# Attention logits as three rounded products, and the key weights' staging moved in the queue

## The chip, the cores and the metric

The kernel runs on one core of a Trainium2 chip. The metric is the device time of one execution in microseconds (us). Before the change three runs gave 1312.15, 1314.40 and 1316.61 us, a median of 1314.4 us. The profile is that of one further execution.

The engines are TensorE (PE; PEld is its weight loading), VectorE (DVE), ScalarE (ACT), GpSimd (POOL) and SyncE (SP), which here only issues DMAs. Each works through a queue of its own in order.

## The reference, cut to what matters

A decoder trunk of two layers on 512 tokens of width 1024, in float32. Layer 0 is a Mamba-2 mixer and a ConvFFN. Then keys and values are projected once. Layer 1 is differential attention (8 heads, two maps of 64 dimensions each, causal) and a second ConvFFN:

```
k_sh, v_sh = rms_norm(kv[..., :1024] per 64, k_norm_g), kv[..., 1024:]
q = rms_norm((rms_norm(x, ln_g) @ q_w) per 64, q_norm_g)
logits = einsum('bqhcd,bkhcd->bhcqk', q, k) / 8 + bias        # c: the two maps
p = softmax(where(causal, logits, -inf))
o = einsum('bhqk,bkhd->bqhd', p[:, :, 0] - lam * p[:, :, 1], v)
```

## The kernel before, in words

Most products are made in a rounded form of float32 (type F32R): an operand is split into a high half, rounded by an ACT copy, and a low half, the rest, made on DVE, and a product of two operands is three matmuls (high by high, high by low, low by high) that add up in one PSUM bank. Weights come as pieces of 1024 columns by 128 partitions: a load on SP, the split, three buffers ahead of PE (`Weights`, `chunk`). Logits, attention values and transposes are plain float32 matmuls.

The order of PE's instructions is written out by hand. The instructions of ACT, DVE, POOL and the DMA queues are put in order by a planner, which issues each once its inputs are expected to be ready. It may place an instruction much earlier than the program has it. `tc.issue_after(i)` keeps what is inside it behind instruction i in the planned order.

**Layer 0's ConvFFN** (`ffn`) works on 22 pairs of a gate block and an up block in three parts (pairs 0 to 5, 6 to 13, 14 to 21). Each part's down projection comes after the first pair of the next part. `plain` makes a pair with full products; `tapped` (L1476) applies the convolution's taps and the silu (L1478). `double` makes two pairs at once with fewer multiplications. Beside it `stage` (L1483), called after each step of parts two and three but the down steps, prepares the keys' weights: `key_weights_in` loads one of eight pieces (L1005, SP) into the single buffer `stage`; two steps later `key_weights_out` scales its two halves on ACT (L1011) and stores it to a scratch in HBM (L1012, issued by ACT). The keys read the scratch after layer 0.

**Attention.** After the q projection of heads 0 to 3 (`qk("q0")`) and the keys (`keys`, seven products per piece, accumulated in `acc`), PE runs a list of steps, `ORDER`. An f step is six matmuls of a filler (v projection, q projection of heads 4 to 7, second v projection, output projection). L makes the logits of two units, a makes the transposes of a unit's weights, v its products with the values, o the turning of a finished head. A unit is one head with query blocks (0, 1), (2) or (3); block i has (i + 1) x 128 key columns. Its two maps lie in partitions 0 to 63 and 64 to 127 and in two PSUM banks. DVE adds the bias and takes the maximum (L1847), ACT makes the exponentials (L1854), and DVE weighs the maps (L1864).

Queries and keys are transposed in `head_norm`, one bank per block of 128 tokens with four heads in it (L1687), and copied to `qT` and `kT` by ACT with the gain (L1689). The four turnings hang in a list `late`, which the projections work off at given steps. `ap` and `kc` are memory pools; the attention's pools `op_` and `up` take the place of `kc` once the keys are made. Four banks (`aux_bank`) go round for transposes, logits and values.

Of the kernel before, what the change touches and what calls it, by code (L numbers as in the profile page):

```python
# [9 lines left out]
F32 = mybir.dt.float32  # L10
# [8 lines left out]
P = 128  # L19
T = 512  # L20
# [25 lines left out]
def trunk_kernel(ctx: ExitStack, tc, x, ssm_ln_g, ssm_in_w, ssm_conv_w, ssm_conv_b, ssm_dt_bias,  # L46
# [19 lines left out]
    def aux_bank(name):  # L66
        return pp.tile([P, T], F32, tag="aux", name=name)
# [497 lines left out]
    def run(gen):  # L565
        for _ in gen:
            pass
# [19 lines left out]
    def chain(*gens):  # L587
        for g in gens:
            yield from g
# [418 lines left out]
    def key_weights_out(n, v):  # L1008
        k0, i = n // 2 * 2, n % 2
        for k in range(2):  # L1010
            act.activation(v[:, k], v[:, k], AF.Copy, scale=c2[:, 32 + k0 + k:33 + k0 + k])  # L1011
        act.dma_start(key_weights(k0, i), v)  # L1012
# [19 lines left out]
    def ffn(l, norm, bp, gnext, nnext):  # L1032
        with (tc.tile_pool(name="ffn_h%d" % l, bufs=1) as hp, tc.tile_pool(name="ffn%d" % l, bufs=1) as fp,
# [441 lines left out]

            def tapped(p, us):  # L1476
                ga = taps(0, p, us[0])
                act.activation(ga, ga, AF.Silu)  # L1478
                return ga, taps(1, p, us[1])

            staged = {"n": 0, "at": 0, "v": None}
# [1 line left out]
            def stage():  # L1483

                staged["at"] += 1
                if staged["v"] and staged["at"] > 1:
                    key_weights_out(*staged["v"])
                    staged.update(v=None, at=0)
                elif not staged["v"] and staged["n"] < KB and staged["at"] > 1:
                    staged.update(v=key_weights_in(fp, staged["n"]), n=staged["n"] + 1, at=0)  # L1490
# [116 lines left out]
    with tc.tile_pool(name="att", bufs=1) as ap, ExitStack() as later:  # L1607
        rts = []
        late = []

        kT = [ap.tile([P, 4, T], F32, name="kT%d" % i) for i in range(2)]
        qT = [ap.tile([P, 4, T], F32, name="qT%d" % i) for i in range(2)]
        vt = [ap.tile([P, D], F32, name="vt%d" % b) for b in range(NT)]

        def key_load(t, j, i, c, **more):
# [51 lines left out]
            act.activation(s, t, AF.Square)  # L1667
            dve.reduce_sum(out[:, b, :], s.rearrange("p (a q) -> p a q", a=8), axis=AX.X)

        def head_norm(key, kn, ss, dst, gcol, where):  # L1670
            rsqrt_act(ss, ap, key, [P, NT, 8], 64)
            def normed():
                for b in range(NT):
                    v = kn[b].rearrange("p (a q) -> p a q", a=8)
                    dve.tensor_tensor(out=v, in0=v, in1=ss[:, b, :].unsqueeze(2).to_broadcast([P, 8, 64]),
                                      op=ALU.mult)

            if key == "q1":
                late.append(((0, 3), normed))
            else:  # L1680
                normed()

            def turned(bs):
                for b in bs:
                    ps = aux_bank("kt%s_%d" % (key, b))
                    for h in range(4):
                        pe.transpose(ps[:, h * P:(h + 1) * P], kn[b][:, h * P:(h + 1) * P], ident)  # L1687
                    v = ps.rearrange("p (h t) -> p h t", h=4)
                    act.activation(dst[:, :, b * P:(b + 1) * P], v if key[0] == "k" else v[:, :, ::-1],  # L1689
                                   AF.Copy, scale=c2[:, gcol:gcol + 1])  # L1690

            for at, bs in zip(where, ((0, 1), (2, 3))):
                late.append((at, lambda bs=bs: turned(bs)))

        def head_sums(key):
            return ap.tile([P, NT, 8], F32, tag="qss", name="ss" + key, bufs=2)

        def qk(key, dst, gcol, where):
            kn, ss = [], head_sums(key)

            def evac(b, ps, rt):
                t = ap.tile([P, T], F32, tag="kn", name="kn%s_%d" % (key, b), bufs=4)
                act.activation(t, ps, AF.Copy, scale=rt[:, b:b + 1])
                squared(key, t, rt, ss, b)
                kn.append(t)

            yield from proj(key, evac)
            head_norm(key, kn, ss, dst, gcol, where)

        def keys(kc):  # L1710

# [2 lines left out]

            def first(i, b, ps):
                acc[i][b] = (ap.tile([P, T], F32, tag="kn", name="key%d_%d" % (i, b), bufs=4) if i
                             else qT[1][:, b, :])
                if ps is not None:
                    act.activation(acc[i][b], ps, AF.Copy)

# [23 lines left out]
            def finish(i, where):  # L1744
                key, ss = "k%d" % (1 - i), head_sums("k%d" % (1 - i))
                for b in range(NT):
                    act.activation(acc[i][b], acc[i][b], AF.Copy, scale=rts[0][:, b:b + 1])
                    squared(key, acc[i][b], rts[0], ss, b)
                head_norm(key, acc[i], ss, kT[1 - i], 48, where)

            for m in SEVEN[1]:
                pss = [(aux_bank if m in "127" else mm_bank)("ps_K%s_%d" % (m, b)) for b in range(2)]
# [34 lines left out]
                        add(acc[0][2 + b], ps, r_)  # L1787
                if m == "3":
                    finish(1, ((4, 0), (4, 2)))
            finish(0, ((0, 1), (0, 3)))  # L1790

        def vproj(key, i):
            def evac(b, ps, rt):
                act.activation(vt[b][:, i * 512:(i + 1) * 512], ps, AF.Copy, scale=rt[:, b:b + 1])
            yield from proj(key, evac)

        PARTS = ((0, 1), (2,), (3,))
        ORDER = ("f f L f f f a f",
# [12 lines left out]
        fl = lambda a: a.rearrange("p a b -> p (a b)")  # L1811
# [1 line left out]
        class Unit:  # L1813
# [9 lines left out]
            def logits(self):  # L1823
                h, tag, st = self.h, self.tag, self.st
                if self.part == 0:
                    st["tb"] = up.tile([P, T], F32, tag="tb", name="tb%d" % h, bufs=2)
                    sync.dma_start(st["tb"], bass.AP(tensor=bd.tensor, offset=h * NBIAS + 1, ap=[[1, P], [1, T]]))
                    st["sm"] = up.tile([P, NT, 2], F32, tag="sm", name="sm%d" % h, bufs=3)
                i2, h4 = h // 4, h % 4
                k = len(self.ii)  # L1830
                mx = up.tile([P, k, 2], F32, tag="mx%d" % k, name="mx" + tag, bufs=3)
                self.sm = st["sm"][:, self.ii[0]:self.ii[-1] + 1, :]
                self.p = [up.tile([P, T], F32, tag="p%d" % m, name="lg%s_%d" % (tag, m), bufs=3)
                          for m in range(2)]
                pss = [aux_bank("lg%s_%d" % (tag, m)) for m in range(2)]
                for j, i in enumerate(self.ii):
                    n = (i + 1) * P
                    c = slice(self.off[j], self.off[j] + n)
                    for m in range(2):
                        rows = slice(64 * m, 64 * (m + 1))  # L1840
                        pe.matmul(pss[m][:, c], qT[i2][rows, h4, i * P:(i + 1) * P], kT[i2][rows, h4, :n],
                                  start=True, stop=True)
                for j, i in enumerate(self.ii):
                    n = (i + 1) * P
                    c = slice(self.off[j], self.off[j] + n)
                    for m in range(2):
                        dve.tensor_tensor_reduce(self.p[m][:, c], pss[m][:, c],  # L1847
                                                 st["tb"][:, (3 - i) * P:], 1.0, 3.0e38,
                                                 ALU.add, ALU.min, mx[:, j, m:m + 1])
                for j, i in enumerate(self.ii):  # L1850
                    n = (i + 1) * P
                    for m in range(2):
                        v = self.p[m][:, self.off[j]:self.off[j] + n]
                        act.activation(v, v, AF.Exp, bias=mx[:, j, m:m + 1], scale=-1.0,  # L1854
                                       accum_out=self.sm[:, j, m:m + 1])
# [103 lines left out]
            run(rest)  # L1959

        with tc.manual_schedule(engines={mybir.EngineType.PE}):
            run(qk("q0", qT[0], 49, (("2", 1), ("5", 0))))
            with tc.tile_pool(name="keys", bufs=1) as kc:
                keys(kc)
            op_ = later.enter_context(tc.tile_pool(name="att_o", bufs=1))
            up = later.enter_context(tc.tile_pool(name="units", bufs=1))
            fill = chain(vproj("v0", 0), qk("q1", qT[1], 49, ((2, 0), (2, 1))), vproj("v1", 1),
                         attn_out(0, None, range(KB)))
            us = []
            for h in range(AH):  # L1970
# [30 lines left out]
            for step in " ".join(ORDER).split():  # L2001
                if step == "L":
                    pair = next(pairs)
                    for u in pair:
                        u.logits()
                    for u in pair:
                        u.weigh()
                else:
                    steps[step]()
            assert next(fill, None) is None  # L2010
# [39 lines left out]
```

## Time and profile before

| | |
|---|---|
| median of three runs | 1314.4 us |
| profiled execution | 1314.86 us, span from first to last instruction 1313.2 us |
| PE | busy 1304.0 us |
| DVE, ACT, POOL | busy 1074.7, 748.0, 184.8 us |
| mean granted TensorE clock | 0.999 of full speed |

A row of the timeline gives start, duration, engine, line, operation, out<-in, shapes and a count where neighbours of one form were merged; in brackets stands idle time of the engine before it and what ended it. Matmuls overlap in the pipeline, so the distance from start to start, not the duration, is what one costs. In the shapes all float32 forms are written f32.

### The profile page before, as it was taken

What the parts mean: (1) busy time and instruction counts of PE and PEld (TensorE: products, weight loads), DVE (VectorE), ACT (ScalarE), POOL (GpSimd) and SP (SyncE); (2) the same over time, 40 slices, a digit from 0 to 9 for tenths busy, and PEclk for the clock granted to TensorE, in tenths of its full rate; (3) what the DMA queues carried; (4) which work ended last, traced back from release to release, by engine and by line L of the source; (5) the groups of instructions that cost most, each with busy time, mean ns of one, the idle gap of its engine ahead of it and who ended that gap; (6) DMA issues with size and microseconds to landing.
All of it is one profiled execution on the core that took longest, in us unless ns stands there. A gap on an engine that the chain in (4) does not pass through costs nothing.

```text
span 1313.2 us, 18936 instructions
## 1 busy us (share of the span) xinstructions
PE 1304.0 (99%) x7059; PEld 1106.4 (84%) x7059; DVE 1074.7 (82%) x1796; ACT 748.0 (57%) x1234; POOL 184.8 (14%) x212
## 2 busy tenths in 40 slices
PE   9999999999999999999999999999999999999998
PEld 8878888888888798999889887877888889988887
DVE  7989878889879876986768878677789977997776
ACT  6696554743367545653445667777656535643442
POOL 5230200300020421020002310000020030020001
PEclk9999999999999999999999999999999999999999
DMA  7553533432366797769337663222233586566325
GB/s 210 154 154 91 151 99 102 145 98 75 105 191 183 182 219 156 154 144 212 101 88 144 175 146 112 81 65 65 63 107 89 145 204 156 141 123 187 99 62 128
DMA packets 198588, 174.18 MB, mean 133 GB/s; under 512 B 7964, under 2 KB 172192, under 8 KB 198496
## 3 DMA queue, kind: packets, MB, share of 16 engines
q1 hardware_dynamic: 164336, 119.69, 30.9%
q0 software_dynamic: 30704, 47.99, 19.0%
q10 hardware_dynamic: 3456, 5.30, 1.2%
q8 instruction: 55, 0.90, 0.3%
q14 instruction: 37, 0.30, 0.1%
HBM read 166.51 MB, written 6.44 MB: 132 GB/s over the span
## 4 chain that ended last, share of the span: by engine, by line
PE 94%; DVE 2%; ACT 2%; DMA 1%; issue 0%; DVEq 0%; ACTq 0%; SPq 0%
PE ps_in L246 5%; PE ps_in L248 5%; PE ps_in L247 5%; PE ps_g L248 4%; PE ps_g L246 4%; PE ps_g L247 4%; PE ps_u L246 4%; PE ps_u L247 4%; PE ps_u L248 4%; PE ps_s L1439 3%; PE ps_s L1444 3%; PE ps_s L1442 3%; PE ps_s L1338 3%; PE ps_s L1341 3%; PE ps_s L1343 3%; PE ps_o L247 2%
## 5 line engine op out<-in xcount | busy, mean ns | idle before, releaser
L246 PE MATMUL ps_in<-xgh,wh_in 128*128 128x512 f32 x304 | 122.9, 404 | 0.0
L196 DVE TENSOR_TENSOR wl_h<-wr_h,wh_h 128x1024 fp32r<-128x1024 f32 x72 | 88.4, 1231 | 40.7 <-ACT wh_h L185 38.1
L248 PE MATMUL ps_in<-xgh,wl_in 128*128 128x512 f32 x304 | 119.7, 394 | 0.0
L247 PE MATMUL ps_in<-xgl,wh_in 128*128 128x512 f32 x304 | 119.2, 392 | 0.0
L248 PE MATMUL ps_g<-xgh,wl_h 128*128 128x512 f32 x288 | 112.9, 392 | 2.2 <-DVE wl_h L196 2.2
L247 PE MATMUL ps_g<-xgl,wh_h 128*128 128x512 f32 x288 | 112.7, 391 | 0.4 <-DVE xgl L1084 0.4
L246 PE MATMUL ps_g<-xgh,wh_h 128*128 128x512 f32 x288 | 113.0, 392 | 0.0
L246 PE MATMUL ps_u<-xgh,wh_h 128*128 128x512 f32 x288 | 112.1, 389 | 0.0
L247 PE MATMUL ps_u<-xgl,wh_h 128*128 128x512 f32 x288 | 112.1, 389 | 0.0
L248 PE MATMUL ps_u<-xgh,wl_h 128*128 128x512 f32 x288 | 112.1, 389 | 0.0
L185 ACT ACTIVATE wh_h<-wr_h 128x1024 fp32r<-128x1024 f32 x72 | 76.2, 1059 | 59.7 <-PE ps_u L247 17.2
L1083 ACT ACTIVATE sh<-vg 128x512 fp32r<-128x512 f32 (+1 forms) x81 | 42.2, 530 | 60.1 <-DVE vg L1160 35.1
L1238 POOL DMA_DIRECT2D wz<-in_ffn_down_w_dram x28 | 33.8, 1229 | 285.9 <-DVE wl_s L1277 125.2
L248 PEld LDWEIGHTS ps_in<-xgh,wl_in 128*128 128x128 f32 x304 | 57.1, 188 | 12.2 <-issue 0.4
L246 PEld LDWEIGHTS ps_in<-xgh,wh_in 128*128 128x128 f32 x304 | 57.2, 188 | 11.6 <-issue 1.3
L247 PEld LDWEIGHTS ps_in<-xgl,wh_in 128*128 128x128 f32 x304 | 57.3, 188 | 11.0 <-issue 0.5
L248 PEld LDWEIGHTS ps_g<-xgh,wl_h 128*128 128x128 f32 x288 | 54.5, 189 | 14.1 <-DVE wl_h L196 2.6
L247 PEld LDWEIGHTS ps_g<-xgl,wh_h 128*128 128x128 f32 x288 | 54.4, 189 | 11.8 <-DVE xgl L1084 0.8
L1444 PE MATMUL ps_s<-sl,wh_s 128*128 128x256 f32 x252 | 64.1, 283 | 0.0
L1442 PE MATMUL ps_s<-sh,wh_s 128*128 128x256 f32 x252 | 64.1, 283 | 0.0
L185 ACT ACTIVATE wh_in<-wr_in 128x1024 fp32r<-128x1024 f32 x39 | 41.2, 1057 | 39.8 <-PE ps_in L247 30.0
L1276 ACT ACTIVATE wh_s<-wz 128x1024 fp32r<-128x1024 f32 (+2 forms) x38 | 37.3, 981 | 46.7 <-PE ps_s L1343 16.5
(512 smaller groups left out, 3795.4 us busy)
## 6 DMA issues: line engine op xcount, KB each, us to landing
wr_h<-in_ffn_up_w_dram SPq DMA_DIRECT2D x60, 512.0 KB, 4.3
wr_in<-in_ssm_in_w_dram SPq DMA_DIRECT2D x40, 512.0 KB, 3.9
wz<-in_ffn_down_w_dram POOLq DMA_DIRECT2D x21, 512.0 KB, 5.8
m<-cumd POOLq DMA_DIRECT2D x16, 512.0 KB, 4.4
wr_out<-in_ssm_out_w_dram SPq DMA_DIRECT2D x16, 512.0 KB, 3.5
wr_s<-in_ffn_down_w_dram SPq DMA_DIRECT2D x13, 512.0 KB, 4.3
wr_h<-in_ffn_up_w_dram SPq DMA_DIRECT2D x24, 256.0 KB, 3.5
wx<-in_ffn_down_w_dram POOLq DMA_DIRECT2D x12, 512.0 KB, 7.2
```

Of the source, the lines that this page charges most:

```text
L185: return act.activation(self.wh[:, :self.n], self.raw[:, :self.n], AF.Copy)
L196: return eng.tensor_tensor(out=self.wl[:, :self.n], in0=self.raw[:, :self.n], in1=self.wh[:, :self.n].bitcast(F32), op=ALU.subtract)
L246: pe.matmul(ps, wh, xh, start=start, stop=False)
L247: pe.matmul(ps, wh, xl, start=False, stop=False)
L248: return pe.matmul(ps, wl, xh, start=False, stop=stop).ins
L1083: act.activation(hi, v, AF.Copy)
L1338: pe.matmul(pss[b], h, ws[q][1][:, cols], start=False, stop=end and q == qs[-1], skip_group_check=more)
L1341: pe.matmul(pss[b], h, ws[q][0][:, cols], start=first and q == qs[0], stop=False, skip_group_check=more)
L1343: pe.matmul(pss[b], w, ws[q][0][:, cols], start=False, stop=False, skip_group_check=more)
L1439: pe.matmul(v[:, b], wl[:, q, cols], h, start=False, stop=q == nq - 1, skip_group_check=not opens or b > 0)
L1442: pe.matmul(v[:, b], wh[:, q, cols], h, start=opens and q + b == 0, stop=False, skip_group_check=not opens or b > 0)
L1444: pe.matmul(v[:, b], wh[:, q, cols], w, start=False, stop=False, skip_group_check=not opens or b > 0)
```

## The change

In `tapped` the silu's instruction is kept, and the scalings and the store of a staged piece are issued behind the newest silu. The logits of a block become three matmuls per map in the rounded form, from high and low halves of queries and keys. Each kind has one high and one low tile for four heads; heads 4 to 7 reuse the place of heads 0 to 3, head by head. So the turning goes head by head (`turn_head`: four transposes, an ACT copy for the high half, a DVE instruction for the low half), and for heads 4 to 7 it becomes steps k4 to k7 and q4 to q7 of `ORDER`. The second half's keys accumulate in the memory of `key_raw` and are normed into the right halves of the value tiles `vt`, which the second v projection writes later.

```diff
@@ tapped, stage
-                act.activation(ga, ga, AF.Silu)
+                state["silu"] = act.activation(ga, ga, AF.Silu).ins
...
-                    key_weights_out(*staged["v"])
+                    with tc.issue_after(state["silu"]):
+                        key_weights_out(*staged["v"])
@@ tiles
-        kT = [ap.tile([P, 4, T], F32, name="kT%d" % i) for i in range(2)]
-        qT = [ap.tile([P, 4, T], F32, name="qT%d" % i) for i in range(2)]
+        turned_by = {n: [ap.tile([P, 4, T], F32R, name=n + "T_" + x) for x in ("hi", "lo")] for n in "kq"}
+        second = {}
@@ head_norm
+        def turn_head(kind, h, src):
+
+            ps = aux_bank("kt%s%d" % (kind, h))
+            for b in range(NT):
+                pe.transpose(ps[:, b * P:(b + 1) * P], src[b][:, h % 4 * P:(h % 4 + 1) * P], ident)
+            g = c2[:, 48:49] if kind == "k" else c2[:, 49:50]
+            v, hi, lo = (t.rearrange("p (b t) -> p b t", b=NT) for t in [ps] + [t[:, h % 4] for t in turned_by[kind]])
+            if kind == "q":
+                v = v[:, :, ::-1]
+            act.activation(hi, v, AF.Copy, scale=g)
+            dve.scalar_tensor_tensor(out=lo, in0=v, scalar=g, in1=hi.bitcast(F32), op0=ALU.mult, op1=ALU.subtract)
...
-            def turned(bs):
-                for b in bs:
-                    ps = aux_bank("kt%s_%d" % (key, b))
-                    for h in range(4):
-                        pe.transpose(ps[:, h * P:(h + 1) * P], kn[b][:, h * P:(h + 1) * P], ident)
-                    v = ps.rearrange("p (h t) -> p h t", h=4)
-                    act.activation(dst[:, :, b * P:(b + 1) * P], v if key[0] == "k" else v[:, :, ::-1],
-                                   AF.Copy, scale=c2[:, gcol:gcol + 1])
-
-            for at, bs in zip(where, ((0, 1), (2, 3))):
-                late.append((at, lambda bs=bs: turned(bs)))
+            if key[1] == "1":
+                second[key[0]] = to
+                return
+            for at, hs in zip(where, ((0, 1), (2, 3))):
+                late.append((at, lambda hs=hs: [turn_head(key[0], h, to) for h in hs]))
@@ keys
-                             else qT[1][:, b, :])
+                             else whole_sums[:, b // 2, 2 * (b % 2):2 * (b % 2) + 2].rearrange("p k t -> p (k t)"))
...
-                head_norm(key, acc[i], ss, kT[1 - i], 48, where)
+                head_norm(key, acc[i], ss, where, None if i else [v[:, T:] for v in vt])
@@ ORDER
-        ORDER = ("f f L f f f a f",
-                 "L f f a v f v f a f",
-                 "L f f a v f v f a f",
-                 "L f f a v f v f o a f",
-                 "L f f a v f f v o a f",
+        ORDER = ("f f f L f f f a f",
                  "L f f a v f v a f",
+                 "L f f k4 a v f v f a f",
+                 "L f f k5 a v f v f o a f",
+                 "L f f a v f o f v a f",
+                 "L f f k6 a v q4 f v a f",
+                 "L f f k7 a v f q5 v o a f",
+                 "L f f a f o q6 v a f f",
+                 "L f f q7 v a f v v a",
                  "L f f a v f v o a f",
-                 "L f f a f o f v a f",
-                 "L f f v a f v v a",
-                 "L f f a v f v o a f",
-                 "L f f a v o f v a",
+                 "L f f a v o v a f",
                  "L f f a v f v a",
                  "f a v f o v")
@@ Unit.logits
-                    for m in range(2):
-                        rows = slice(64 * m, 64 * (m + 1))
-                        pe.matmul(pss[m][:, c], qT[i2][rows, h4, i * P:(i + 1) * P], kT[i2][rows, h4, :n],
-                                  start=True, stop=True)
+                    for z, (q, k) in enumerate(((qh, kh), (ql, kh), (qh, kl))):
+                        for m in range(2):
+                            rows = slice(64 * m, 64 * (m + 1))
+                            pe.matmul(pss[m][:, c], q[rows, h4, i * P:(i + 1) * P], k[rows, h4, :n],
+                                      start=z == 0, stop=z == 2)
```

## Rows read from the trace of the kernel before

**Rows 1.** The page: busy time and instructions of each engine.
```profile
PE 1304.0 (99%) x7059; PEld 1106.4 (84%) x7059; DVE 1074.7 (82%) x1796; ACT 748.0 (57%) x1234; POOL 184.8 (14%) x212
```

**Rows 2.** Timeline of PE around 433 us.
```profile
433.74 0.39 PE L247 MATMUL ps_g<-xgl,wh_h 128*128 128x512 f32 x1
436.33 0.79 PE L248 MATMUL ps_g<-xgh,wl_h 128*128 128x512 f32 x1 [2.21 <-DVE wl_h L196]
436.92 0.63 PE L246 MATMUL ps_g<-xgh,wh_h 128*128 128x512 f32 x1
437.35 0.63 PE L247 MATMUL ps_g<-xgl,wh_h 128*128 128x512 f32 x1
...
439.75 0.40 PE L247 MATMUL ps_g<-xgl,wh_h 128*128 128x512 f32 x1
```

**Rows 3.** Timeline of PE around 407 us.
```profile
406.95 0.39 PE L246 MATMUL ps_g<-xgh,wh_h 128*128 128x512 f32 x1
407.75 0.50 PE L247 MATMUL ps_g<-xgl,wh_h 128*128 128x512 f32 x1 [0.41 <-DVE xgl L1084]
408.08 0.39 PE L248 MATMUL ps_g<-xgh,wl_h 128*128 128x512 f32 x1
408.31 0.40 PE L246 MATMUL ps_u<-xgh,wh_h 128*128 128x512 f32 x1
```

**Rows 4.** Windows: stretch, then busy PE, PEld, DVE, ACT, POOL, clock, DMA.
```profile
433.00:440.00 7.00, 4.79 (x15) 3.49 (x15) 5.55 (x10) 5.60 (x9) 3.75 (x3) 0.76 0.74 227
```

**Rows 5.** Timeline of ACT around 433 us.
```profile
432.56 1.34 ACT L1011 ACTIVATE stage<-stage,c 128x512 f32<-128x512 f32 x2 [2.79 <-DMA stage<-in_kv_w_dram]
433.80 0.61 ACT L1478 ACTIVATE vg<-vg 128x512 f32<-128x512 f32 x1
```

**Rows 6.** Timeline of DVE around 433 us.
```profile
429.84 0.74 DVE L1068 SCALAR_TENSOR_TENSOR vg<-ps_g,cf,vg 128x510 f32<-128x510 f32 x1
...
431.15 1.22 DVE L1084 TENSOR_TENSOR sOl<-wz,sOh 128x1024 fp32r<-128x1024 f32 x1
434.45 0.69 DVE L1160 TENSOR_TENSOR vg<-vg,vu 128x512 f32<-128x512 f32 x1 [2.08 <-ACT vg L1478]
435.06 1.22 DVE L196 TENSOR_TENSOR wl_h<-wr_h,wh_h 128x1024 fp32r<-128x1024 f32 x1
```

**Rows 7.** The staged piece's load on SP; waits of its scalings (total, times, longest).
```profile
427.59 0.37 SPq L1005 DMA_DIRECT2D stage<-in_kv_w_dram  x1
...
ACT stage L1011 <- DMA stage<-in_kv_w_dram: 6.5, 2, 3.7
```

**Rows 8.** Timeline of PE in a logit group, asked in narrow windows.
```profile
818.25 0.70 PE L1841 MATMUL lg<-kT,qT 64*128 64x512 f32 x2
...
818.78 0.70 PE L1841 MATMUL lg<-kT,qT 64*128 64x512 f32 x4
...
819.21 0.61 PE L1841 MATMUL lg<-kT,qT 64*128 64x128 f32 x6
...
819.43 0.60 PE L1841 MATMUL lg<-kT,qT 64*128 64x256 f32 x4
```

**Rows 9.** Windows: the first steps of part two.
```profile
490.00:508.00 18.00, 18.00 (x104) 15.86 (x103) 11.30 (x15) 9.83 (x15) 3.86 (x3) 1.00 0.93 198
```

**Rows 10.** Timeline of PE: rounded matmuls of 256 columns; transposes.
```profile
464.77 0.28 PE L1444 MATMUL ps_s<-sl,wh_s 128*128 128x256 f32 x1
464.89 0.28 PE L1442 MATMUL ps_s<-sh,wh_s 128*128 128x256 f32 x1
...
808.32 1.03 PE L1687 MATMUL ktk<-ident,key 128*128 128x128 f32 x8
809.11 0.48 PE L1649 MATMUL ps_v<-wh_v,xgh 128*128 128x512 f32 x1
```

**Rows 11.** The output's low half (line view); windows of the attention.
```profile
L1911 DVE SCALAR_TENSOR_TENSOR ol<-oT,c,oh x8: 741/746/752, 853.3 to 944.8; 128x512 fp32r<-128x512 f32 x8
...
818.20:898.00 79.80, 79.45 (x458) 62.49 (x459) 56.75 (x183) 60.43 (x157) 0.00 (x0) 1.00 0.25 71
```

More of the change, by code (lines that the diff above doesn't have):

```diff
@@ L1668, in squared, with head_norm @@
             dve.reduce_sum(out[:, b, :], s.rearrange("p (a q) -> p a q", a=8), axis=AX.X)
-        def head_norm(key, kn, ss, dst, gcol, where):
+        def turn_head(kind, h, src):
[8 more added lines that the diff above has]
+            dve.scalar_tensor_tensor(out=lo, in0=v, scalar=g, in1=hi.bitcast(F32), op0=ALU.mult, op1=ALU.subtract)
+        def head_norm(key, kn, ss, where, to=None):
             rsqrt_act(ss, ap, key, [P, NT, 8], 64)
+            to = to or kn
             def normed():
                 for b in range(NT):
-                    v = kn[b].rearrange("p (a q) -> p a q", a=8)
-                    dve.tensor_tensor(out=v, in0=v, in1=ss[:, b, :].unsqueeze(2).to_broadcast([P, 8, 64]),
+                    v, o = (t[b].rearrange("p (a q) -> p a q", a=8) for t in (kn, to))
+                    dve.tensor_tensor(out=o, in0=v, in1=ss[:, b, :].unsqueeze(2).to_broadcast([P, 8, 64]),
                                       op=ALU.mult)
@@ L1681, in head_norm, with qk @@
                 normed()
-            def turned(bs):
-                for b in bs:
-                    ps = aux_bank("kt%s_%d" % (key, b))
-                    for h in range(4):
-                        pe.transpose(ps[:, h * P:(h + 1) * P], kn[b][:, h * P:(h + 1) * P], ident)
-                    v = ps.rearrange("p (h t) -> p h t", h=4)
-                    act.activation(dst[:, :, b * P:(b + 1) * P], v if key[0] == "k" else v[:, :, ::-1],
-                                   AF.Copy, scale=c2[:, gcol:gcol + 1])
-            for at, bs in zip(where, ((0, 1), (2, 3))):
-                late.append((at, lambda bs=bs: turned(bs)))
+            if key[1] == "1":
[3 more added lines that the diff above has]
+                late.append((at, lambda hs=hs: [turn_head(key[0], h, to) for h in hs]))
         def head_sums(key):
             return ap.tile([P, NT, 8], F32, tag="qss", name="ss" + key, bufs=2)
-        def qk(key, dst, gcol, where):
+        def qk(key, where=()):
             kn, ss = [], head_sums(key)
@@ L1707, in qk @@
             yield from proj(key, evac)
-            head_norm(key, kn, ss, dst, gcol, where)
+            head_norm(key, kn, ss, where)
         def keys(kc):
@@ L1789, in keys @@
                     finish(1, ((4, 0), (4, 2)))
-            finish(0, ((0, 1), (0, 3)))
+            finish(0, ())
         def vproj(key, i):
@@ L1828, in logits @@
                     st["sm"] = up.tile([P, NT, 2], F32, tag="sm", name="sm%d" % h, bufs=3)
-                i2, h4 = h // 4, h % 4
+                (kh, kl), (qh, ql) = (turned_by[n] for n in "kq")
+                h4 = h % 4
                 k = len(self.ii)
@@ L1961, in trunk_kernel @@
         with tc.manual_schedule(engines={mybir.EngineType.PE}):
-            run(qk("q0", qT[0], 49, (("2", 1), ("5", 0))))
+            run(qk("q0", (("2", 1), ("5", 0))))
             with tc.tile_pool(name="keys", bufs=1) as kc:
@@ L1966, in trunk_kernel @@
             up = later.enter_context(tc.tile_pool(name="units", bufs=1))
-            fill = chain(vproj("v0", 0), qk("q1", qT[1], 49, ((2, 0), (2, 1))), vproj("v1", 1),
+            fill = chain(vproj("v0", 0), qk("q1"), vproj("v1", 1),
                          attn_out(0, None, range(KB)))
@@ L2007, in trunk_kernel @@
                         u.weigh()
+                elif step[0] in "kq":
+                    turn_head(step[0], int(step[1]), second[step[0]])
                 else:
```

## The prediction

> **What bounds the kernel now.** I read the page first. TensorE (PE) is busy for 99% of the span [rows 1], so a change counts only by what it does to PE's steps and to the places where PE waits. Next I stepped through PE's matmuls and marked each start that comes later than its form allows. Outside the first 12 us and the scan, one place stands out: in layer 0's ConvFFN a matmul starts 2.59 us after the one before it, and the following ones are 0.43 us apart [rows 2], where the same form elsewhere steps by 0.23 us [rows 3]. The granted clock is 0.76 over those 7 us, which is a stretch at the lower of the two levels, 1.2 GHz, after PE had stood idle [rows 4]. From 433.74 to 439.75 PE takes 6.01 us for nine steps that would take 9 x 0.23 = 2.07: **3.94 us are lost here**.
>
> The queues say why. VectorE (DVE) had finished the low half of x at 432.37, then waited 2.08 us for a silu (L1478), and only then made the piece wl_h that PE lacked [rows 6]. ScalarE (ACT) ran that silu at 433.80, although its input was ready at 430.58 (429.84 + 0.74, [rows 6]): ahead of it in ACT's queue stood two scalings of a staged key weight (L1011), which waited 2.79 us for their load [rows 5]. The load was issued at 427.59 [rows 7]. So the key weights' staging, which nobody needs before the keys, holds up layer 0.
>
> The last view is the logits. A logit matmul is float32 and shows as two records. Its two maps use partitions 0 to 63 and 64 to 127, and two matmuls of 512 columns together last 0.70 us [rows 8]: they run side by side.
>
> **Part 1, the scalings behind a silu.** In program order, the first staged piece goes out after the two halves of pair 7, so the silu it is now tied to is pair 7's, and the others follow pairs 7, 10, 10, 11, 14, 16 and 18. Pairs 3 to 5 are what PE works on around 433; pair 7 comes after the first down projection, at about 490. So all 16 scalings, the eight stores that ACT issues and, through the single staging buffer, seven of SP's eight loads leave the stretch up to 440 for 490 to 670. What is late next at 433: silu at 430.6 to 431.2, DVE's 1.22 us piece still ends at 432.37, then L1160 (0.69, stepping 0.61) and wl_h (1.22) end at 432.28 + 0.61 + 1.22 = 434.1. PE wanted it at 433.97, so about 0.3 us stay, too short (I judge) to drop the clock: a wait of 0.57 us at 407 left the steps at 0.23 to 0.33 [rows 3]. Saved: 3.94 - 0.3 = **3.6 us**. That earlier wait at 407 (0.80 - 0.23 = 0.57 us, for DVE's xgl) also hangs on an ACT that had idled for a staged load: two such waits between 400 and 440 make 6.5 us [rows 7]. I count 0.6 of it with the small one behind it as saved: **0.6 us**.
>
> Where they go, each piece adds two scalings (1.34 us of ACT together, [rows 5]), a 0.5 MB load on SP and a 0.5 MB store. ACT is busy for 9.8 of 18 us there and PE waits for nothing; the DMA share is 0.93 in the first stretch [rows 9]. The cover is the weights' lead over PE. If it holds, the cost is nothing. If not: pieces 2 and 4 follow the same silu as the piece before them, so their scalings can again stand in ACT's queue before the load has landed, and each can cost what it costs today, 3.94 us. Both ends are kept, 0 and 7.9; I take 0.3, since the silu rule clears six of eight.
>
> **Part 2, three products for one.** Per head there are four blocks of 128, 256, 384 and 512 columns, and each block's pair of maps ran two float32 records. Read from starts: 512 columns 818.78 to 819.21, 0.43 per record; 128 columns two records from 819.21 to 819.43, 0.11 each; 256 columns then about 0.215; 384 by the line between, 0.32 [rows 8]. A head takes 2 x (0.11 + 0.215 + 0.32 + 0.43) = 2.15 us. The rounded form (fp32r) steps by 0.23 at 512 columns [rows 3] and by 0.12 at 256 [rows 10]; 384 between them is 0.17. At 128 columns no fp32r matmul is in the trace. The nearest row is a transpose, one record of 128 columns with its own weight load: eight from 808.32 to 809.11, 0.10 each [rows 10]; at the other end, each product could take what a whole float32 one takes, 2 x 0.11 = 0.22. I take 0.115. Three products: 3 x (0.115 + 0.12 + 0.17 + 0.227) = 1.90 us. Saved 0.25 us per head, **2.0 us** in eight heads; with 0.22 at 128 columns, 3 x 0.105 x 8 = 2.5 us worse, a loss of 0.5. That the pairs run side by side in fp32r too is taken from the float32 pairs; otherwise a head takes 3.8 us and the logits lose 13.2. The first load of each of 12 logit groups, and the change of array shape, stay. The Trainium skill, in TensorE: Matmul & The Clock Gate, Part 3: Packing small matmuls, says that a weight load overlaps a running matmul only where the row groups differ. By that rule each of a half's three products would show its load, and so would today's records; the trace disagrees for these, since 0.43 us for 512 columns is the same per column as 0.11 for 128 [rows 8]. What the rule would make of the time is the fifth rival.
>
> **Part 3, turning by head.** The transposes stay 64, in 16 banks; ACT's copies stay 16 and now write the high half. New are 16 DVE instructions for the low half, each like the output's (L1911) at 0.746 us [rows 11]: 11.9 us of DVE, four of them while the keys are made, some 9 in the attention units. DVE is busy there for 56.75 of 79.8 us [rows 11]; with 9 us more it is at 82%. A bank is now held until DVE has read it. In the list of places, the tightest turn is q5: a value product, an output, a turn and one f step (six matmuls of 0.23, 1.4 us) lie between it and head 5's logits; q4 has two f steps, the others a whole line. ACT's copy (0.67 like a scaling, [rows 5]) and DVE's 0.75 fit. The first logits come one f later, which covers DVE's extra work on key heads 0 to 3. The second key half is normed into the right halves of vt, written by the last value projection only after k7, and accumulates in key_raw, which frees the attention's memory later: a bias load on SP could wait for it, with q's weight loads behind it; they have some 10 us to spare. PE is busy for 79.45 of 79.80 us there, so there is next to no wait to win. Bounds: 0 and 5 us (half of DVE's 9 us exposed); I take **0.3 us** lost.
>
> **Sum.** 3.6 + 0.6 - 0.3 + 2.0 - 0.3 = 5.6 us off. The profiled execution took 1314.86 us (span 1313.2), 0.46 over the median of three, 1314.4, whose runs spread over 4.5 us; so I take the gain off the median: **1308.8 us**, 0.43% less. A time counts as no change here within 0.3%, that is 1310.5 to 1318.3.
>
> **Rivals.**
> *A stall moves.* ACT is again blocked on a staged load, now among the double units, where ACT also empties PE's banks. For it: two such waits in 40 us today, the longest 3.7 us [rows 7], and a full DMA stretch. Against: PE waits for nothing there now. One stall of 3.94: 1312.7; two: 1316.7. Chance 0.15.
> *Short columns at the old price.* 128-column products at 0.22: 1308.8 + 2.5 = 1311.3. For it: no row shows them; against: a transposed 128-column record at half that. Chance 0.09.
> *DVE becomes late.* The 9 us in attention show half: 1308.8 + 4.5 = 1313.3. For it: 82% is a mean, and single lines will be fuller; against: today's 71% leaves PE whole, and the new turns are spread over six lines. Chance 0.06.
> *The fp32r halves don't run side by side.* Place: the new loop over three products. Six products in turn per block take 6 x 0.632 = 3.8 us per head for 2.15: 13.2 us lost in place of 2.0 won, 1308.8 + 2.0 + 13.2 = 1324.0. It outweighs part 1 from the point at which the logits cost 3.6 us more than today. For it: no fp32r pair is in the trace. Against: float32 pairs share the array [rows 8], and the halves differ in nothing else. Chance 0.06.
> *Each product pays for its load.* A load that isn't hidden costs about 0.1 us (the first record of a pair of 512 columns takes 0.53 us to the second, the next 0.43, [rows 8]); 12 products per head, of which nine at 0.1 and three at 0.05, make 8.4 us more: 1317.2. Against: from the second record on, today's reloads don't show. Chance 0.04. The rule of the Trainium skill named in part 2 speaks for this one.
> *The silu tie does nothing.* If the tied silu were one that stands behind the scalings anyway, 433 would keep its stall: 1308.8 + 4.2 = 1313.0. Against: the program order above. Chance 0.03.
>
> **How the numbers follow.** The forecast has 0.57, with its own range of 1306.0 to 1311.0. Faster by over 0.3%: nearly nine tenths of the forecast's cases and a little of the second rival, rounded up for small gains uncounted, 0.56. Slower by over 0.3%: the fourth rival and a rest for orders that I can't see, 0.09. The remainder, 0.35, is no change. The range reaches down to 1305.5 and up to 1315.0, which leaves out the fourth and fifth rivals and two moved stalls.
>
> **What would show it.** After: no matmul gap over 0.6 us and clock 1.00 at 433 to 440; L1011 between about 500 and 670; PE whole from 490 to 670; fp32r logit records in pairs starting a few ns apart, 192 in all where a matmul is one record, with blocks of 512 stepping 0.23. The logit group of 512, 128 and 256 columns that starts at 818.25 should shrink by about 0.13 us. Wrong would be: a new PE wait for a wh or wl in 500 to 560, starts of a pair 0.2 us apart, or PE waiting for turned keys' low halves.

## The result, and the profile after

The changed kernel takes **1317.49 us** (median; 1316.84 to 1318.67) against 1312.64 for the kernel before on the same chip (1311.78 to 1316.61): a ratio of 1.0033, 95% interval 1.0023 to 1.0044. It is slower by 4 to 5 us (0.33%), where 1308.8 was forecast and the range ended at 1315.0. The profiled execution took 1316.84 us, its span 1315.1.

Windows of the kernel after (columns as in [rows 4]): the old stall, the new one, and the attention.

```profile
433.00:440.00 7.00, 7.00 (x32) 5.81 (x31) 7.00 (x12) 3.01 (x5) 4.14 (x3) 1.00 1.06 218
530.00:547.00 17.00, 11.34 (x59) 9.80 (x58) 16.03 (x27) 14.37 (x26) 2.56 (x2) 0.80 0.81 185
818.20:898.00 79.80, 79.80 (x502) 65.83 (x501) 64.87 (x206) 61.61 (x168) 0.00 (x0) 1.00 0.24 77
```

At 433 PE is now whole at full clock (7.00 of 7.00 us, clock 1.00, against 4.79 and 0.76 in [rows 4]). What was won is lost 100 us later: from 530 to 547 PE is busy for 11.34 of 17 us, at a mean clock of 0.80. PE's timeline there (start, us, engine, line, tiles; in brackets the idle time and what ended it):

```profile
530.84 0.39 PE L248 MATMUL ps_g<-xgh,wl_h 128*128 128x512 f32 x1
531.94 0.38 PE L1185 MATMUL ps_U<-sEh,wh_U 128*128 128x256 f32 x1 [0.72 <-ACT wh_U L1152]
...
533.52 0.74 PE L1190 MATMUL ps_U<-sEh,wl_U 128*128 128x256 f32 x4 [0.36 <-DVE wl_U L1153]
...
538.18 0.39 PE L1185 MATMUL ps_U<-xgh,wh_U 128*128 128x256 f32 x1 [2.49 <-ACT wh_U L1152]
...
541.48 1.22 PE L1190 MATMUL ps_U<-xgh,wl_U 128*128 128x256 f32 x4 [2.09 <-DVE wl_U L1153]
542.50 0.41 PE L1185 MATMUL ps_U<-xgh,wh_U 128*128 128x256 f32 x1
542.71 0.41 PE L1187 MATMUL ps_U<-xgl,wh_U 128*128 128x256 f32 x1
```

Four waits for split weights, by starts 0.88, 0.52, 2.65 and 2.25 us beyond the normal step, and behind them steps of 0.21 us for 256 columns where 0.12 is normal: the lower level of the clock, as in [rows 2, 4]. With these slow steps up to 547 (some 2.7 us) and a wait of 0.49 at 557, about 9.5 us go. All four hang on wh_U or wl_U, so ACT's queue is the next view:

```profile
515.80 1.34 ACT L1011 ACTIVATE stage<-stage,c 128x512 f32<-128x512 f32 x2 [2.45 <-DMA stage<-in_kv_w_dram]
517.17 0.37 ACTq L1012 DMA_DIRECT2D ks<-stage  x1
517.58 1.06 ACT L1152 ACTIVATE wh_U<-wr_U 128x1024 fp32r<-128x1024 f32 x1 [0.44 <-ACT stage L1011]
...
519.55 1.06 ACT L185 ACTIVATE wh_h<-wr_h 128x1024 fp32r<-128x1024 f32 x1 [0.25 <-PE ps_U L1187]
529.30 1.34 ACT L1011 ACTIVATE stage<-stage,c 128x512 f32<-128x512 f32 x2 [8.68 <-DMA stage<-in_kv_w_dram]
530.54 0.40 ACT L1083 ACTIVATE sh<-vg 128x256 fp32r<-128x256 f32 x1
...
530.85 1.04 ACT L1152 ACTIVATE wh_U<-wz 128x1024 fp32r<-128x1024 f32 x1
...
537.08 1.04 ACT L1152 ACTIVATE wh_U<-wz 128x1024 fp32r<-128x1024 f32 x1
```

ACT stands for **8.68 us** before the scalings of the fourth staged piece, the second one behind pair 10's silu; the weight that PE needs at 531 is split right behind them. The waits of 500 to 560 (total, times, longest, as in [rows 7]) hold two more of them, and the load left SP's queue late:

```profile
ACT stage L1011 <- DMA stage<-in_kv_w_dram: 14.2, 3, 8.7
```

```profile
522.06 0.37 SPq L1005 DMA_DIRECT2D stage<-in_kv_w_dram  x1
```

With one staging buffer this load waits for piece three's store, issued at 517.17; it starts at 522.06 and lands 7.2 us later, where the load of [rows 7] took about 5. The staged loads also hold up the weights' loads behind them in SP's queue (by up to 11.6 us there), but from 500 to 560 the staged load is the only one that ACT waits for: no weight's load came too late.

### The profile page after: what moved, and what is told of

It reads as the page before. It is cut to its first block, busy times and chain, and to the rows that moved or that the text cites. A ratio compares the mean times of both kernels' runs of the same rounds, so it can differ in the third digit from the quotient of the medians.

```text
span 1315.1 us, 19092 instructions
## 1 busy us (share of the span) xinstructions
PE 1302.6 (99%) x7123; PEld 1110.6 (84%) x7123; DVE 1083.9 (82%) x1812; ACT 746.1 (57%) x1234; POOL 187.5 (14%) x212
## 4 chain that ended last, share of the span: by engine, by line
PE 94%; DMA 2%; DVE 2%; ACT 1%; issue 0%; DVEq 0%; ACTq 0%; SPq 0%
PE ps_in L246 5%; PE ps_in L248 5%; PE ps_in L247 5%; PE ps_u L246 5%; PE ps_u L247 5%; PE ps_g L248 5%; PE ps_u L248 5%; PE ps_g L247 5%; PE ps_g L246 5%; PE ps_s L1439 3%; PE ps_s L1444 3%; PE ps_s L1442 3%; PE ps_s L1338 3%; PE ps_s L1341 3%; PE ps_s L1343 3%; PE ps_o L247 2%
## 5 line engine op out<-in xcount | busy, mean ns | idle before, releaser
L248 PEld LDWEIGHTS ps_u<-xgh,wl_h 128*128 128x128 f32 x288 | 54.4, 189 | 11.3
L247 PEld LDWEIGHTS ps_u<-xgl,wh_h 128*128 128x128 f32 x288 | 54.4, 189 | 11.2
L246 PEld LDWEIGHTS ps_u<-xgh,wh_h 128*128 128x128 f32 x288 | 54.4, 189 | 11.2
```

The lines of the kernel that those rows point to most:

```text
L246: pe.matmul(ps, wh, xh, start=start, stop=False)
L247: pe.matmul(ps, wh, xl, start=False, stop=False)
L248: return pe.matmul(ps, wl, xh, start=False, stop=stop).ins
```

## Experiments

Each was timed beside the kernel before, whose median moves by up to 2 us between sets of runs; so ratios to it are given too, each with its 95% interval.

**Which part costs.** The kernel before with part 1 alone:

```
-  act.activation(ga, ga, AF.Silu)
+  state["silu"] = act.activation(ga, ga, AF.Silu).ins
...
-  key_weights_out(*staged["v"])
+  with tc.issue_after(state["silu"]):
+      key_weights_out(*staged["v"])
```

> The kernel before with part 1 alone (the scalings behind a silu). Theory, blocked queue: in the kernel after, ScalarE waits 8.68 us for the load of the fourth staged piece, whose scalings stand in its queue behind the same silu as the third's, and TensorE then loses about 10 us among the double units. All of the loss is part 1's, so this kernel lacks only what the attention gained (1.8 us from the keys' start to the last turn): 1317.5 + 1.8 = 1319.3 us, 1318.0 to 1320.5. Rival, the other parts cost: then part 1 keeps its 4 us and this takes 1308.5.

Measured: 1318.54 us, ratio 1.0027 (1.0016 to 1.0038). The other way round, the kernel after with exactly these lines taken back:

> The kernel after without part 1: three rounded products and turning by head alone. Blocked queue: 1312.6 - 1.8 = 1310.8 us, 1310.0 to 1312.0, with the waits at 407 and 433 back as they were. Rival, the other parts cost: 1317 or more.

Measured: 1311.78 us, ratio 0.9985 (0.9973 to 0.9997). All of the loss is part 1's; parts 2 and 3 gain. The wait at 433 is back, but not the lower clock:

```profile
432.83 0.39 PE L247 MATMUL ps_g<-xgl,wh_h 128*128 128x512 f32 x1
436.31 0.50 PE L248 MATMUL ps_g<-xgh,wl_h 128*128 128x512 f32 x1 [3.09 <-DVE wl_h L196]
436.64 0.39 PE L246 MATMUL ps_g<-xgh,wh_h 128*128 128x512 f32 x1
436.87 0.40 PE L247 MATMUL ps_g<-xgl,wh_h 128*128 128x512 f32 x1
```

**Blocked queue, transfers, or a lead given back.** One piece per silu, in the kernel after:

```
-  if staged["v"] and staged["at"] > 1:
-      with tc.issue_after(state["silu"]):
+  if staged["v"] and staged["at"] > 1 and state.get("silu"):
+      with tc.issue_after(state.pop("silu")):
```

> The kernel after, but each silu lets out one staged piece only, so the fourth piece follows pair 14's silu and no longer pair 10's. Blocked queue: no wait of ScalarE that reaches TensorE, neither at 433 nor at 530: 1317.5 - 9.8 = 1307.7 us, 1306.5 to 1309.5. Rival, traffic: the staged loads and stores still fall among the double units' weights, a little thinner; about half of the loss stays, 1312 to 1315. Rival, lead given back: TensorE, now 5.9 us earlier at 453, meets the end of its weights whatever the staging does; 1313 to 1317.

Measured: **1307.98 us**, ratio 0.9949 (0.9937 to 0.9962). Its window, and ACT's queue at the place:

```profile
530.00:547.00 17.00, 17.00 (x113) 15.62 (x112) 16.45 (x25) 11.46 (x20) 1.28 (x1) 1.00 0.74 156
```

```profile
520.87 1.06 ACT L185 ACTIVATE wh_h<-wr_h 128x1024 fp32r<-128x1024 f32 x1 [0.89 <-PE ps_U L1187]
...
523.80 1.06 ACT L1152 ACTIVATE wh_U<-wz 128x1024 fp32r<-128x1024 f32 x1 [0.20 <-PE ps_U L1187]
...
528.92 1.05 ACT L1152 ACTIVATE wh_U<-wz 128x1024 fp32r<-128x1024 f32 x1
```

The same wh_U is made at 523.80 instead of 530.85, and PE is whole. PE's rows show when it uses that wh_U and the next one:

```profile
532.37 0.28 PE L1185 MATMUL ps_U<-sEh,wh_U 128*128 128x256 f32 x1
...
535.25 0.28 PE L1185 MATMUL ps_U<-xgh,wh_U 128*128 128x256 f32 x1
```

The second kernel leaves the scaling out and keeps the bytes:

```
-  sync.dma_start(v, w)          # at the load's place
...
-  act.activation(v[:, k], v[:, k], AF.Copy, scale=...)   # two of them
-  act.dma_start(key_weights(k0, i), v)
+  act.dma_start(v, w)
+  act.dma_start(key_weights(k0, i), w)
```

> The kernel after with the scaling of the key weights left out: at the places of the scalings ScalarE only issues a load of the piece and a copy of it from memory to memory, and waits for neither. The bytes moved and their places stay about as they were, the waits of ScalarE are gone. Blocked queue: 1307.7 us, 1306.0 to 1309.5, TensorE whole from 500 to 560. Rival, traffic: 1316 to 1318, with TensorE's stalls still there. Rival, lead given back: 1313 to 1317.

Measured: 1308.31 us, ratio 0.9951 (0.9939 to 0.9964). Windows:

```profile
490.00:530.00 40.00, 40.00 (x257) 36.50 (x257) 29.11 (x42) 23.25 (x35) 6.44 (x5) 1.00 0.99 253
530.00:547.00 17.00, 17.00 (x115) 15.73 (x114) 17.00 (x26) 11.23 (x18) 1.28 (x1) 1.00 0.74 145
```

The transfers are fuller than in the kernel after (DMA share 0.99 from 490 to 530, where it had 0.84), all transfers of the first four pieces are issued by 517, and PE loses nothing. Traffic and a lead given back both fall; it is ACT's standing in its queue. This kernel also takes the staged loads out of SP's queue; that these don't cost in this stretch is read from the kernel after, where ACT waits for no other load.

**The price of the wait.** Three kernels change which stores hold a load up; the silus stay as in the kernel after. n counts pieces from 0; the first has `n == 2`, the others `n < 2` and `n < 3`:

```
-  act.dma_start(key_weights(k0, i), v)
+  act.dma_start(key_weights(k0, i), w_cols(kv_w, k0, 2, i * 512, 512)[0] if n == 2 else v)
```

> The kernel after, with the silus as they are, but the third staged piece's store reads the weight from memory and no longer the staging buffer (so that piece stays unscaled). The fourth load then waits for the third piece's scalings only and can start at about 517.2 instead of 522.06. If it takes its 7.2 us again it lands at 524.4, and ScalarE, free at 520.6, waits 3.8 us instead of 8.68. Theory, blocked queue with a lead: the pieces two and three make ScalarE wait 3.1 and 2.5 us at no cost to TensorE, so the lead of the split weights is some 3 us, and a wait of 3.8 costs 0 to 2 us: 1307.7 to 1310.0. Rival, price in proportion: 3.8 of 8.68 is 44% of 9.8 us: 1312. Rival, the transfers are full and the load lands at 527 or later whenever it starts: 1314 or more.

Measured: 1312.28 us, ratio 0.9989 (0.9980 to 0.9998). The load started at 517.67 and landed at 523.7; ACT waited 4.49 us. My lead of 3 us was wrong: this is the rival's figure. I then took it for one account on which all waits draw.

> The kernel after, with the stores of the first and second staged pieces reading the weight from memory (these two pieces stay unscaled), the third's as it is. The loads of pieces two and three can then start one store earlier, so ScalarE no longer waits for them (3.1 and 2.4 us in the kernel after), while piece four's load still waits for the third's store and leaves some 7 to 8.5 us of wait. Theory, one account: the split weights' lead over TensorE is some 5 us in this stretch and all three waits draw on it (14.2 us of waits cost 9.5, 9.8 us cost 4.3 with the third store apart), so this costs about 3: 1311 us, 1309.5 to 1312.5. Rival, only the fourth wait counts, at about 1 us per us: 1316, 1314.5 to 1317.5.

Measured: 1317.27 us, ratio 1.0022 (1.0013 to 1.0031).

> The same with the first three stores reading from memory (three pieces stay unscaled): all four loads start one store earlier, the silus are as in the kernel after, and the fourth wait shrinks to some 2 to 4.5 us with no wait before it. One account: inside the lead of 5 us, 1307.6 to 1309.0. Rival, only the fourth wait counts: 1310 to 1312.5. Rival, two pieces behind one silu are bad in themselves: 1314 or more.

Measured: 1312.43 us, ratio 0.9984 (0.9975 to 0.9993). ACT's scalings of pieces three and four, first with two stores apart, then with three:

```profile
514.67 1.32 ACT L1011 ACTIVATE stage<-stage,c 128x512 f32<-128x512 f32 x2
529.53 1.34 ACT L1011 ACTIVATE stage<-stage,c 128x512 f32<-128x512 f32 x2 [8.75 <-DMA stage<-in_kv_w_dram]
```

```profile
514.54 1.32 ACT L1011 ACTIVATE stage<-stage,c 128x512 f32<-128x512 f32 x2
524.09 1.33 ACT L1011 ACTIVATE stage<-stage,c 128x512 f32<-128x512 f32 x2 [4.84 <-DMA stage<-in_kv_w_dram]
```

The account falls too. Piece three's wait (2.45 us in the kernel after, 2.14 with the third store apart) is gone in both, and nothing is gained by it. Piece two's wait is not gone, against what was expected: it is 3.03 us in the kernel after and 3.21, 3.94 and 3.40 in these three, so they don't show what it costs. What the time follows is the fourth wait: over the 1307.98 of one piece per silu, 4.49 us of it cost 4.3, 4.84 cost 4.5, 8.68 cost 9.5 and 8.75 cost 9.3 (by the ratios 5.3, 4.6, 11.0 and 9.6). That is about 1 us per us, with the lower clock in the two long ones. It is no rule, though: in the two short ones the scalings also stand ahead of wh_h, which ACT splits behind them, while in the two long ones wh_h is split before the wait (519.55 in the kernel after). ACT's next row, and PE's waits, with the third store apart:

```profile
524.99 1.04 ACT L185 ACTIVATE wh_h<-wr_h 128x1024 fp32r<-128x1024 f32 x1
```

```profile
526.08 0.50 PE L246 MATMUL ps_g<-xgh,wh_h 128*128 128x512 f32 x1 [0.33 <-ACT wh_h L185]
...
527.34 0.50 PE L248 MATMUL ps_g<-xgh,wl_h 128*128 128x512 f32 x1 [0.53 <-DVE wl_h L196]
...
537.71 0.74 PE L1190 MATMUL ps_U<-xgh,wl_U 128*128 128x256 f32 x4 [1.24 <-DVE wl_U L1153]
...
552.21 0.39 PE L1185 MATMUL ps_U<-sEh,wh_U 128*128 128x256 f32 x1 [1.06 <-ACT u L1195]
```

"Two behind one silu" is no harm in itself: the kernel without the scalings has that too, and takes 1308.31.

**Another engine for the scalings.** Part 1 taken back, `act.activation` of the scalings replaced by `pool.tensor_scalar(..., op0=ALU.mult)`, and the store issued by POOL.

> The kernel after without the silus' tie, the scalings and stores of the staged key weights done by GpSimd instead of ScalarE, and so back in the stretch up to 440. Blocked queue: what costs is only that ScalarE, which splits every weight, stands behind a load; GpSimd has nothing in that stretch that TensorE needs soon, so the stalls at 407 and 433 go without a tie: 1308 to 1309.5 us. Rival, any queue that waits costs, or GpSimd's scalings slow VectorE's work beside them: 1311.5 or more.

Measured: 1327.91 us, ratio 1.0115 (1.0100 to 1.0131): the rival, by far. POOL's timeline, and PE's where it waits for it:

```profile
373.19 3.26 POOL L1011 TENSOR_SCALAR stage<-stage,c 128x512 f32<-128x512 f32 x2 [4.01 <-DMA stage<-in_kv_w_dram]
376.43 1.28 POOL L605 TENSOR_TENSOR nacc_f<-nacc_f,nsq_f 128x512 f32<-128x512 f32 x1
...
385.63 3.11 POOL L1011 TENSOR_SCALAR stage<-stage,c 128x512 f32<-128x512 f32 x2 [4.13 <-DMA stage<-in_kv_w_dram]
388.72 1.25 POOL L605 TENSOR_TENSOR nacc_f<-nacc_f,nsq_f 128x512 f32<-128x512 f32 x1
```

```profile
390.85 1.09 PE L552 MATMUL tr_nf<-ident,nacc_f 128*128 128x128 f32 x4 [7.67 <-DVE nacc_f L605]
```

The sums of the norm (L605) stand in POOL's queue between the pieces; the last of them is made on DVE, which waits 6.69 us for POOL's at 388.72, and PE needs it. At 433 PE then waits 6.71 us for wl_h, whose raw weight ACT awaits for 9.35: its load is behind the staged one in SP's queue, and that waits for the stores of POOL (ACT's row, then SP's waits from 400 to 437).

```profile
436.45 1.06 ACT L185 ACTIVATE wh_h<-wr_h 128x1024 fp32r<-128x1024 f32 x1 [9.35 <-DMA wr_h<-in_ffn_up_w_dram]
```

```profile
SPq L1005 <- DMA ks<-stage: 43.6, 4, 13.7
```

**The one new wait in attention.** In the kernel after, a second value product now stands right behind an output's transposes and waits for `at`:

```profile
924.18 0.60 PE L1916 MATMUL oT<-ident,ot 128*128 128x128 f32 x4
925.34 0.94 PE L1894 MATMUL po<-vt,at 128*128 128x128 f32 x6 [0.56 <-ACT at L1884]
```

```
-  "L f f a v o v a f",
+  "L f f a v o f v a",       (on top of one piece per silu)
```

> One piece per silu, and in the list of places the tenth line goes back from 'o v a f' to 'o f v a', as before the change, so that one step of the output projection lies again between an output and the value product behind it. Theory: the 0.70 us for which TensorE waits there (916.4 in the run with one piece per silu) for the weights' transposed copies goes; 1308.0 - 0.6 = 1307.4 us, 1306.8 to 1308.2. Rival: the wait comes back one line later, as that line lost its step; 1308.0.

Measured: 1307.88 us, ratio 0.9960 (0.9948 to 0.9973). Its trace has the wait no more and its span is 0.9 us shorter (1306.2 for 1307.1), but the two ratios don't tell the kernels apart. Both beat the kernel before by 0.4 to 0.5%, and the kernel after by some 9.5 us.

## Why the prediction was wrong, point by point

**The cover of part 1: the step that failed.** It said of the moved scalings: "The cover is the weights' lead over PE. If it holds, the cost is nothing"; pieces 2 and 4 "can again stand in ACT's queue before the load has landed", and "I take 0.3, since the silu rule clears six of eight". Piece four did stand there, 8.68 us long, and cost 9.5 us. Two errors are in it. First, the value was chosen by counting pieces that the rule clears; one that it doesn't clear is enough, and piece three, behind a silu of its own, waited too (2.45 us): a silu says nothing of where a load is. Second, the price of a stall was taken from the old place, 3.94 us for a wait of 2.79. The length of a wait is set by the chain that it ends: scaling, store (4.8 us), load (7.2 us among the double units' transfers), scaling.

The cover was there, but shorter than that chain. Piece two stood 3.03 us and PE lost nothing (busy 40.00 of 40 us from 490 to 530). With one piece per silu wh_U is ready 7.5 us before PE uses it (523.80 + 1.06 for 532.37), the next wh_U 5.3 us (528.92 + 1.05 for 535.25). In the kernel after, the fourth wait puts the first off to 530.85, and PE waits 0.88 us for it. ACT and DVE then work off what has piled up (busy for 14.37 and 16.03 of the 17 us), and the next wh_U starts at 537.08, 8.2 us later than with one piece per silu; there, and at its low half, PE waits 2.65 and 2.25 us. So one wait uses up the cover, and the weights behind it pay. With the third store apart it is wh_h and wl_h that come behind the scalings; they have leads of 5.0 and 3.1 us with one piece per silu, and PE waits for both. Why these waits, with the later ones at 537 and 552, again come to about the length of ACT's wait isn't settled.

So *A stall moves* was the right rival, with its place, at 0.15 and 1312.7; priced by the chain it would have said some 1317.5 (1308.8 + 8.7).

**The stall at 433 and the wait at 407.** Right: both are gone, the 0.3 us that were to stay as well (the prediction's own sum, 434.1 for 433.97, gives 0.1). Part 1 was to give 3.6 + 0.6 - 0.3 = 3.9 us; from part 1 taken back to one piece per silu, timed side by side, it is 1311.78 - 1307.98 = 3.8. That these agree so closely is partly luck: with part 1 taken back the wait at 433 is longer (3.25 us for 2.37), and the 1.6 us of lower clock that the 3.94 hold are not there.

**The logits.** Right: 2.0 us were forecast; from start to start the 12 logit groups take 19.97 us before and 17.78 after, 2.2 less. The group of 512, 128 and 256 columns that was to shrink by 0.13 takes 1.58 us (823.38 to 824.96) for 1.71 ([rows 8], 818.25 to 819.96 by the full timeline):

```profile
823.38 0.50 PE L1851 MATMUL lg<-kT_hi,qT_hi 64*128 64x512 f32 x2
823.72 0.39 PE L1851 MATMUL lg<-kT_hi,qT_lo 64*128 64x512 f32 x2
823.95 0.40 PE L1851 MATMUL lg<-kT_lo,qT_hi 64*128 64x512 f32 x2
824.18 0.22 PE L1851 MATMUL lg<-kT_hi,qT_hi 64*128 64x128 f32 x2
824.24 0.27 PE L1851 MATMUL lg<-kT_hi,qT_lo 64*128 64x128 f32 x2
824.35 0.28 PE L1851 MATMUL lg<-kT_lo,qT_hi 64*128 64x128 f32 x2
824.47 0.33 PE L1851 MATMUL lg<-kT_hi,qT_hi 64*128 64x256 f32 x2
...
824.96 0.50 PE L1650 MATMUL ps_q<-wh_q,xgh 128*128 128x512 f32 x1
```

Every x2 is the two maps side by side, 0.23 us per product at 512 columns and 0.29 for the three at 128, so the rivals of short columns, of halves in turn and of paid loads, at the prices that the prediction gave them, are all out. The Trainium skill (TensorE: Matmul & The Clock Gate, Part 3: Packing small matmuls) says in its list of what overlaps that a weight load overlaps a running matmul only where the row groups differ. By that each product would show its load; at 512 columns none shows behind the first product (0.23 us a step, as in [rows 3]). At 128 columns the steps of 0.11 are more than a quarter of 0.23, so up to some 0.05 us of a load may show there.

**Turning by head.** About right: DVE's 64.87 us of 79.80 (81%, 82% forecast; 56.75 in [rows 11]) and PE whole. The cost is the 0.7 us wait that a change of the list takes away, less 0.4 of an older one, at 862 in the kernel before. The attention with the keys gained 1.8 us by the traces, forecast 1.7.

With one piece per silu the forecast of 1308.8 would have stood (1307.98, a gain of 0.51% where 0.43% was forecast).

## What to carry to other kernels

Before moving work that waits for a transfer in an in-order queue, follow the chain that ends its wait (buffer, store, load) at the new place, and take a wait's own length there as its price to begin with, not what it cost where it was. An order after an instruction is no order after a transfer: let each release one piece, as here, and see that the gap covers the chain. Before giving such work to an idle engine, read what else is in that engine's queue.

## What the runs showed of the hardware

A wait of PE of 2.37 us at 433 was followed by the lower clock in the kernel before [rows 2, 4], one of 3.25 us at the same place, with part 1 taken back, was not. In the kernel after, the wait of 2.65 us at 538 was followed by full steps (0.12 us at 256 columns) and the one of 2.25 at 541 by slow ones (0.21). No profile here shows why; at 433 it makes the stall's price differ by 1.6 us between executions of nearly the same work.
